# Where the input norm's weights are multiplied in: onto W_in by GpSimd, or onto the transposed rows by VectorE

## The chip, the core and the metric

The kernel runs on one core of a Trainium2 chip. The metric is the device time of one execution in microseconds.

## The reference

Two layers of an encoder trunk, on one sequence of 512 rows of 1024 numbers. What the change touches is the first step of a layer:

```python
h = rmsnorm(x, attn_norm_g[l])          # x * rsqrt(mean(x*x) + eps) * g
proj = einsum('bsd,de->bse', h, w_in)   # 1024 x 2464 columns for all mixers
aq, ak, av, bq, bk, bv, cq, ckv, ckr = split(proj)
kv = einsum('bsr,re->bse', rmsnorm(ckv, kv_norm_g), w_ukv)
vc = kv[..., C_NOPE_DIM:]               # values of the latent heads
```

Sixteen heads follow (six dilated, five differential, five latent), an output projection added to x, and a layer of 16 expert networks that each take 64 rows. The product of h with W_in does not depend on where the vector g is multiplied in: on W_in's rows or on the columns of x.

## The kernel before

A layer is one call of `attention` and then the router and the experts. `attention` loads W_in in seven pieces (`plan`) into three ring slots and works on it in 22 chunks. Chunks 0 to 13 are feature-major: up to 128 columns of W_in are the stationary operand and the 512 transposed rows stream past them, 24 passes of 128x512. Chunks 14 to 21 are token-major and make the values of the dilated and differential heads.

To reach the accuracy of full float32 with the faster format, both operands are cut in a high and a low part. `split` (L330 to L343) cuts a chunk of W_in: ScalarE casts it (L339), VectorE subtracts the cast from the original (L340). `turn_x` (L345 to L353) transposes a tile of x on TensorE into PSUM (L349), half a tile a bank; ScalarE casts it to `xh` (L352), VectorE subtracts to `xl` (L353). Each chunk is the sum of three products: high by high, high weights by low rows, low weights by high rows.

The vector g lies in `gcol`, one number a partition for each of the eight blocks of 128 inputs. `weigh` (L321 to L328) multiplies it onto a chunk of W_in in place, on GpSimd, two chunks ahead of its split. The factor of a row, 1/rms, is made by `row_norms` (squares on ScalarE, L359; the statistic `v` on VectorE, L362; a power on GpSimd, L176) and multiplied in later, when results are read.

Behind each feature-major chunk VectorE, GpSimd and ScalarE rotate it: `raw` (L404) reads PSUM, a shuffle (L406) and a product with the sines (L409) run on VectorE, a product with the cosines (L408) on GpSimd, then the sum `roped` (L410), the cast `hi` (L461) and the difference `lo` (L462). The latent heads need norms of their own columns: `c_sums` and `c_scale` (L450 writes `cqn`), hooked behind chunks 4 and 6. `c_values`, hooked behind chunk 7, makes the latent values from `cqn` (L455) and copies them out (L456). The up-projection of the first latent head (L530 to L532) follows chunk 8.

TensorE, VectorE, ScalarE, GpSimd and SyncE (SP) each run their instructions in a fixed order that the scheduler makes when the program is built; an instruction that waits holds up all behind it on its engine. `heat` issues matmuls on the identity, whose results nothing reads, between the transposes. PSUM has eight banks, handed out in turn. SP issues the loads of W_in and the stores of the rotated parts.

In the expert stage all weights are streamed from HBM, 1408 KB at a time, into tiles that lie where attention's tiles lay.

Of the kernel before, what the change touches and what calls it, by code (L numbers as in the profile page):

```python
# [11 lines left out]
F32 = mybir.dt.float32  # L12
# [5 lines left out]
ALU = mybir.AluOpType  # L18
# [4 lines left out]
P = 128  # L23
S = 512
# [3 lines left out]
KD = D // P  # L28
# [28 lines left out]
EARLY = [[(0, 1)], [(1, 1), (2, 1)], [(3, 1)], [(4, 1)], [(5, 1)], [(6, 1)], [(7, 1)], [], []]  # L57
END_ON = 'avavav'
MARK_AT = 6
FIRST_MARKS = 2  # L60
SCATTER_AT = (2, 4)
HALVED = 8
# [29 lines left out]
PB = 9  # L92
# [37 lines left out]
def body(ctx, tc, x_in, pos, w_in, w_uq, w_ukv, w_out, w_gate, w_up, w_down, gatt, gfin, params, consts, band, sel, out):  # L130
    nc = tc.nc
# [7 lines left out]
    def nm(s):  # L139
        uid[0] += 1  # L140
        return f"{s}_{uid[0]}"

    def bank():
        return pp.tile([P, 512], F32, tag="ps", name=nm("ps"))
# [13 lines left out]
    gcol = cp.tile([P, L, KD], F32, name="gcol")  # L158
# [97 lines left out]
    def attention(l, ap, wk, op):  # L256
# [5 lines left out]
        ukv = ap.tile([P, 5, P], F32, name="ukv")  # L262
# [14 lines left out]
        xl = [wk.tile([P, 4, S], F32R, tag="st", bufs=4, name=nm("xl")) for _ in range(2)]  # L277
# [14 lines left out]
        chunks = [(gi, cols, range(KD)) for gi, (_, _, parts) in enumerate(plan) for cols in parts]  # L292
        feature_major = len(chunks)
        chunks += [(gi, ((0, plan[gi][1]),), range(k, k + 2)) for gi in (5, 6) for k in range(0, KD, 2)]
        loaded = []

        def fetch():
            if len(loaded) < len(plan):
                c0, n, _ = plan[len(loaded)]
                v = slot(f"s{(len(loaded) + 2) % RING}")[:, : KD * n].rearrange("p (k f) -> p k f", k=KD)  # L300
                cuts = (0, 128, n) if not loaded else (0, n)
                for a, b in zip(cuts, cuts[1:]):
                    tc.keep_in_program_order(nc.sync.dma_start(v[:, :, a:b], w_in[l, :, c0 + a : c0 + b].rearrange("(k p) f -> p k f", p=P)))
                    if l == 0 and not loaded and a == 0:
                        for t in range(NT):
                            tc.keep_in_program_order(nc.sync.dma_start(x[:, t, :], x_in[t * P : (t + 1) * P, :]))
                loaded.append(v)
# [10 lines left out]
        nc.sync.dma_start(bandt, band)  # L318
        fetch()

        def weigh(i):  # L321

            if i < len(chunks):
                gi, cols, ks = chunks[i]
                for a, m in cols:
                    v = loaded[gi][:, ks[0] : ks[-1] + 1, a : a + m]
                    g = gcol[:, l, ks[0] : ks[-1] + 1].unsqueeze(2).to_broadcast([P, len(ks), m])
                    tc.keep_in_program_order(nc.gpsimd.tensor_tensor(v, v, g, op=ALU.mult))  # L328

        def split(i):  # L330
            gi, cols, ks = chunks[i]
            if i > 0 and chunks[i - 1][0] != gi and gi + 2 >= len(loaded):
                fetch()
            n = sum(m for _, m in cols)
            w = wk.tile([P, 2 * KD * P], F32R, tag=f"pt{SPLIT_IN[i]}", bufs=1, name=nm("w"))[:, : 2 * len(ks) * n].rearrange("p (c k f) -> p c k f", c=2, k=len(ks))
            o = 0
            for a, m in cols:
                src = loaded[gi][:, ks[0] : ks[-1] + 1, a : a + m]
                nc.scalar.copy(w[:, 0, :, o : o + m], src)  # L339
                nc.vector.tensor_tensor(w[:, 1, :, o : o + m], src, w[:, 0, :, o : o + m].bitcast(F32), op=ALU.subtract)  # L340
                o += m
            weigh(i + 2)
            return w, o  # L343

        def turn_x(t):  # L345
            for h in range(2):
                pt = bank()
                for k in range(4):
                    nc.tensor.transpose(pt[:, k * P : (k + 1) * P], x[:, t, (h * 4 + k) * P : (h * 4 + k + 1) * P], ident)  # L349
                pv = pt.rearrange("p (k s) -> p k s", k=4)  # L350
                hv = xh[:, h * 4 : h * 4 + 4, t * P : (t + 1) * P]
                nc.scalar.copy(hv, pv)  # L352
                nc.vector.tensor_tensor(xl[h][:, :, t * P : (t + 1) * P], pv, hv.bitcast(F32), op=ALU.subtract)  # L353

        def row_norms():
            ss = wk.tile([P, 8], F32, tag="rr", bufs=RB, name=nm("ss"))[:, :NT]
# [8 lines left out]
        def spread(r):  # L365

            b = bank()
            for t in range(NT):
                nc.tensor.transpose(b[:, t * P : (t + 1) * P], r[:, t : t + 1].to_broadcast([P, P]), ident)
            nc.scalar.copy(rb, b)  # L370

        def heat(n):

            if n:
                b = bank()
                for _ in range(n):
                    nc.tensor.matmul(b[:, :P], ident, ident, start=True, stop=True)

        weigh(0)
        if l > 0:  # L380
            weigh(1)
            ready = split(0)
        for t in range(NT):
            heat(START[l][t])
            turn_x(t)
        if l == 0:
            weigh(1)
            ready = split(0)
        heat(START[l][NT])
        rstd = row_norms()  # L390
# [21 lines left out]
        cqn = [cqn2[:, 0], tab_c[0:64, 0], cqn2[:, 1]]  # L412
# [39 lines left out]
        def c_values():  # L452
            for t in range(NT):
                pv = bank()
                nc.tensor.matmul(pv[:, :320].rearrange("p (h c) -> p h c", h=5), cqn[2][:, t * P : (t + 1) * P], ukv[:, :, 64:128], start=True, stop=True)  # L455
                nc.scalar.copy(vC[:, t, :], pv[:, :320])  # L456

        def halves(roped):
# [267 lines left out]
                events[n].pop(0)[2]()  # L726
            events.pop(n, None)

        hooks = {4: c_sums, 5: get_lam, 6: c_scale, 7: c_values}
        hooks.update({i: lambda i=i: step(i - feature_major) for i in range(8, feature_major)})  # L730

        pump(100)
# [1 line left out]
        for i in range(len(chunks)):  # L734
            w, m = ready
            if i < feature_major:
                b = bank()
                passes = ((0, lambda k: xh[:, k, :]), (0, lambda k: xl[k // 4][:, k % 4, :]), (1, lambda k: xh[:, k, :]))
                order = [(j, k) for j in range(3) for k in range(KD)] if i == 0 else [(j, k) for k in range(KD) for j in range(3)]
                for n, (j, k) in enumerate(order):  # L740
                    nc.tensor.matmul(b[:m], w[:, passes[j][0], k, :m], passes[j][1](k), start=(n == 0), stop=(n == 3 * KD - 1))  # L741
            else:
                ks = chunks[i][2]
                if ks[0] == 0:
                    acc = [bank() for _ in range(NT)]
                for kk, k in enumerate(ks):
                    for t in range(NT):
                        q = slice(t * P, (t + 1) * P)
                        for j, (c, xs) in enumerate(((0, xh[:, k, q]), (1, xh[:, k, q]), (0, xl[k // 4][:, k % 4, q]))):
                            nc.tensor.matmul(acc[t][:, :m], xs, w[:, c, kk, :], start=(k == 0 and j == 0), stop=(k == KD - 1 and j == 2))  # L750
                    if kk == 0:
                        step(i - feature_major)
            if i + 1 < len(chunks):
                ready = split(i + 1)
            if i == 2:
                tab_ab = wk.tile([P, 4, S], F32, tag="pt1", bufs=1, name="tab_ab")
                tabs += [tab_ab[:, 0], tab_ab[:, 1], tab_ab[:, 2], tab_ab[:, 3], tab_c[:, 0], tab_c[:, 1]]
                if l == 0:
                    make_tables(tabs, *sines())
                else:  # L760
                    for q in range(6):
                        rows = slice(0, P) if q < 4 else slice(64, 96)
                        nc.scalar.dma_start(tabs[q][rows], tab_d[q, rows])
            if i < feature_major:
                held.append((posts[i], b))
                if i == 1:
                    spread(rstd)
                if i > 0:
                    for fn, b in held:
                        fn(b)  # L770
                    held = []
            elif ks[-1] == KD - 1:
                dst = vB if chunks[i][0] == 5 else vA
                for t in range(NT):
                    nc.scalar.activation(dst[:, t, :], acc[t][:, :m], AF.Copy, scale=rstd[:, t : t + 1])
            if i in hooks:
                hooks[i]()
        late = op.tile([P, 16, 256], F32R, tag="big", name="oh")
# [82 lines left out]
    for l in range(L):  # L861
        with ExitStack() as es:
            ap = es.enter_context(tc.tile_pool(name=f"at{l}", bufs=1, reuse_waits="tile"))
            wk = es.enter_context(tc.tile_pool(name=f"wk{l}", bufs=2, reuse_waits="tile"))
            op = es.enter_context(tc.tile_pool(name=f"op{l}", bufs=1, side="right", reuse_waits="tile"))
            product, work = attention(l, ap, wk, op)
            spots = {}

# [180 lines left out]
            t = NT - 1  # L1049
# [33 lines left out]
        with tc.tile_pool(name=f"fx{l}", bufs=1, reuse_waits="tile") as fx, tc.tile_pool(name=f"fw{l}", bufs=2, side="right", reuse_waits="tile") as fw:  # L1083
# [129 lines left out]
            for p in range(8):  # L1213
                acc = []
                for w in (w_gate, w_up):
                    bs = [bank() for _ in cuts]
                    acc.append(bs)
                    for k in range(KD):
# [7 lines left out]
                        if w is w_gate and k in SCATTER_AT and pending is not None:  # L1226
                            scatter(*pending, 2 * SCATTER_AT.index(k))
                        if w is w_up and k == FIRST_MARKS and p == 0:
                            ohs[0] = marks(0)
                        if w is w_gate and k == MARK_AT and p < 7:  # L1230
                            ohs[p + 1] = marks(p + 1)
# [3 lines left out]
                for g, u, (q0, qn) in zip(acc[0], acc[1], cuts):  # L1235
                    hv = hh[:, :, q0 : q0 + qn].rearrange("p j q -> p q j")
# [14 lines left out]
                for lo in range(0, NJ * D, FF):  # L1251
# [3 lines left out]
                    while e < hi:  # L1255
                        j, h = e // D, e % D // 512
# [143 lines left out]
```

## Time and profile before

| | us |
|---|---|
| median of three runs | 1974.07 |
| lowest and highest run | 1973.97, 1975.56 |
| the profiled execution, its own time | 1974.58 |
| its span, from the first to the last instruction | 1972.8 |

| engine | busy us | share of the span | instructions |
|---|---|---|---|
| TensorE (PE), matmuls | 1754.5 | 89% | 8894 |
| VectorE (DVE) | 739.9 | 38% | 1467 |
| ScalarE (ACT) | 425.0 | 22% | 881 |
| GpSimd (POOL) | 290.8 | 15% | 276 |

The shares are means over stages that differ. The projection and the heads of layer 0 lie in the first 340 us, those of layer 1 between about 985 and 1310 us; the expert stages between and behind them move 420 GB/s or more for most of their time. A line like L340 is line 340 of the kernel before.

### The profile page before, as it was taken

To read this page: it belongs to the slowest core of one execution; us is meant where nothing else is said; L and a number is where in the kernel's file an instruction comes from. 1 tells how busy PE (TensorE), PEld (TensorE's weight loads), DVE (VectorE), ACT (ScalarE), POOL (GpSimd) and SP (SyncE) were. 2 spreads that over 40 slices of the span, in tenths; PEclk is the share of its full clock that TensorE was granted. 3 is DMA by queue.
4 is the path that set the end of the run, shared out by engine and by line. 5 is a ranking of instruction groups with operands and counts; after the bars stand their busy time and mean duration, and the time that the engine had idled before them with its cause. 6 is when DMAs were issued, how large, how long until landed. Compare 5 with 4: busy or idle time off the path is not lost.

```text
span 1972.8 us, 22329 instructions
## 1 busy us (share of the span) xinstructions
PE 1754.5 (89%) x8894; PEld 918.0 (47%) x8894; DVE 739.9 (38%) x1467; ACT 425.0 (22%) x881; POOL 290.8 (15%) x276
## 2 busy tenths in 40 slices
PE   8889999898998988888898899998998988888887
PEld 6667666433333333333386756753333433333323
DVE  7886966111111111211178778551211211211112
ACT  4226972000000000000042379411000000000001
POOL 4552431000000000000055344200000000000000
PEclk9999999999999999999999999999999999999999
DMA  6755548899999999999947546488999999999995
GB/s 220 197 164 91 121 142 322 317 402 423 424 425 424 425 424 425 424 423 425 406 128 224 141 82 158 161 334 346 425 425 424 424 425 424 425 425 424 425 424 245
DMA packets 102473, 646.72 MB, mean 328 GB/s; under 512 B 11009, under 2 KB 28161, under 8 KB 53217
## 3 DMA queue, kind: packets, MB, share of 16 engines
q1 hardware_dynamic: 88336, 606.34, 76.7%
q0 software_dynamic: 11968, 35.02, 7.6%
q10 hardware_dynamic: 2064, 3.93, 0.6%
q8 instruction: 70, 1.15, 0.2%
q14 instruction: 35, 0.28, 0.0%
HBM read 616.55 MB, written 27.39 MB: 326 GB/s over the span
## 4 chain that ended last, share of the span: by engine, by line
DMA 39%; PE 37%; DVE 14%; issue 5%; ACT 3%; POOL 1%; SPq 0%; DVEq 0%; ACTq 0%; POOLq 0%
DMA xslot<-in_w_up_dram 13%; PE ps L1222 10%; DMA xslot<-in_w_gate_dram 10%; PE ps L1259 8%; DMA xslot<-in_w_down_dram 7%; PE ps L840 4%; DMA rows<-xrow_d,slots 3%; DMA slot<-in_w_gate_dram 3%; DMA slot<-in_w_down_dram 3%; PE ps L750 2%; PE ps L741 2%; PE ps L659 2%; PE ps L642 2%; DVE sm L591 1%; DVE sw L409 1%
## 5 line engine op out<-in xcount | busy, mean ns | idle before, releaser
L1222 PE MATMUL ps<-xslot,xe 128*64 128x506 f32 (+1 forms) x2400 | 515.8, 575 | 25.5 <-DMA xslot<-in_w_up_dram 13.3
L1222 PEld LDWEIGHTS ps<-xslot,xe 128*64 128x64 f32 x2400 | 167.0, 140 | 347.3 <-issue 288.5
L1259 PE MATMUL ps<-xslot,hx 128*64 128x512 f32 (+3 forms) x1392 | 248.6, 506 | 22.3 <-DMA xslot<-in_w_down_dram 18.4
L1238 DVE TENSOR_TENSOR hx<-ps,hx 128x506 f32<-128x506 f32 (+1 forms) x48 | 42.9, 957 | 473.9 <-PE ps L1222 473.9
L1259 PEld LDWEIGHTS ps<-xslot,hx 128*64 128x64 f32 x1392 | 94.2, 137 | 164.5 <-issue 123.4
L1189 ACT ACTIVATE hx<-ps,gates 128x512 fp32r<-128x512 f32 x32 | 20.2, 683 | 674.7 <-PE ps L1259 674.7
L1169 POOL DMA_INDIRECT rows<-xrow_d,slots x14 | 13.8, 984 | 985.2 <-DVE oh L1162 913.7
L1190 DVE SCALAR_TENSOR_TENSOR hx<-ps,gates,hx 128x512 fp32r<-128x512 f32 x32 | 22.6, 747 | 344.6 <-ACT hx L1189 344.6
L1222 PE MATMUL ps<-slot,xe 128*64 128x506 f32 (+1 forms) x648 | 141.8, 573 | 7.7 <-DMA slot<-in_w_gate_dram 6.0
L741 PE MATMUL ps<-xh,w 128*128 128x512 f32 (+1 forms) x448 | 142.6, 400 | 3.1 <-DVE w L340 2.4
L1200 DVE TENSOR_TENSOR x<-ps,x 128x512 f32<-128x512 f32 x112 | 69.6, 684 | 161.9 <-PE ps L1198 161.9
L598 ACT ACTIVATE P<-ps,sm 128x512 f32<-128x512 f32 x168 | 116.4, 703 | 41.1 <-DVE sm L591 40.0
L1170 ACT ACTIVATE rows<-rows,slots 128x1024 f32<-128x1024 f32 x14 | 16.1, 1147 | 446.0 <-DMA rows<-xrow_d,slots 446.0
L328 POOL TENSOR_TENSOR slot<-slot,gcol 128x1024 f32<-128x1024 f32 (+4 forms) x46 | 88.1, 1929 | 119.8 <-PE ps L1275 109.8
L741 PEld LDWEIGHTS ps<-xh,w 128*128 128x128 f32 (+1 forms) x448 | 83.3, 187 | 25.9 <-DVE w L340 3.3
L1222 PEld LDWEIGHTS ps<-slot,xe 128*64 128x64 f32 x648 | 45.3, 139 | 93.6 <-issue 75.8
L1177 PE MATMUL ps<-ident,rows 128*128 128x128 f32 x112 | 26.7, 417 | 66.5 <-ACT rows L1170 66.5
L741 PE MATMUL ps<-xl,w 128*128 128x512 f32 (+1 forms) x224 | 85.7, 393 | 0.0
L591 DVE TENSOR_REDUCE sm<-ps 128x1 f32<-128x512 f32 x120 | 78.9, 681 | 8.1 <-PE ps L576 5.7
L642 PE MATMUL ps<-ident,P 128*128 128x128 f32 x512 | 78.0, 275 | 0.3 <-ACT P L598 0.3
L1259 PE MATMUL ps<-slot,hx 128*64 128x512 f32 (+3 forms) x400 | 71.6, 497 | 6.2 <-DMA slot<-in_w_down_dram 4.7
L750 PE MATMUL ps<-w,xh 128*128 128x320 f32 (+1 forms) x256 | 65.9, 342 | 10.4 <-DVE w L340 10.4
(280 smaller groups left out, 2299.1 us busy)
## 6 DMA issues: line engine op xcount, KB each, us to landing
xslot<-in_w_gate_dram SPq DMA_DIRECT2D x100, 1408.0 KB, 26.2
xslot<-in_w_up_dram SPq DMA_DIRECT2D x100, 1408.0 KB, 27.1
xslot<-in_w_down_dram SPq DMA_DIRECT2D x100, 1408.0 KB, 27.0
slot<-in_w_gate_dram SPq DMA_DIRECT2D x28, 1408.0 KB, 27.0
slot<-in_w_down_dram SPq DMA_DIRECT2D x28, 1408.0 KB, 27.0
slot<-in_w_up_dram SPq DMA_DIRECT2D x26, 1408.0 KB, 27.4
slot<-in_w_in_dram SPq DMA_DIRECT2D x8, 1536.0 KB, 6.8
st<-bst_d POOLq DMA_DIRECT2D x40, 256.0 KB, 4.7
```

The source lines that it names most:

```text
L328: tc.keep_in_program_order(nc.gpsimd.tensor_tensor(v, v, g, op=ALU.mult))
L591: nc.vector.tensor_reduce(mn, ps, axis=AX.X, op=ALU.min)
L598: nc.scalar.activation(e, ps, AF.Exp, bias=mn, scale=-1.0, accum_out=lcol)
L642: nc.tensor.transpose(b[:, kc * P : (kc + 1) * P], e[:, kc * P : (kc + 1) * P], ident)
L659: nc.tensor.matmul(o[64 * i : 64 * i + 64], heads[2 * m + i][4][:, kc, :], pts[i][:, kc, :], start=(kc == 0), stop=(kc == NT - 1))
L741: nc.tensor.matmul(b[:m], w[:, passes[j][0], k, :m], passes[j][1](k), start=(n == 0), stop=(n == 3 * KD - 1))
L750: nc.tensor.matmul(acc[t][:, :m], xs, w[:, c, kk, :], start=(k == 0 and j == 0), stop=(k == KD - 1 and j == 2))
L840: nc.tensor.matmul(blocks[t][1 + h], o, w[h], start=(i == 0), stop=(i == 3 * KD - 1))
L1200: nc.vector.tensor_tensor(xv, b, xv, op=ALU.add)
L1222: tc.keep_in_program_order(nc.tensor.matmul(b[64 * i : 64 * i + 64, : qn * NJ], xe[:, k, 64 * i : 64 * i + 64], ws[i][:, q0 * NJ : (q0 + q ...
L1238: nc.vector.tensor_tensor(hv, u[:, : qn * NJ].rearrange("p (q j) -> p q j", j=NJ), hv, op=ALU.mult)
L1259: tc.keep_in_program_order(nc.tensor.matmul(bs[h][64 * i : 64 * i + 64, e % 512 : e % 512 + z - e], hT[:, j, 64 * i : 64 * i + 64], ws[i][ ...
```

## The change

The multiplication by g leaves GpSimd and W_in: `weigh` and its calls go. `turn_x` multiplies g onto the transposed rows instead: VectorE reads the PSUM bank, multiplies and writes a new SBUF tile `gx`; ScalarE's cast and VectorE's subtraction then both read `gx`. The first chunk takes its three products in another order, low weights ahead of low rows. `c_values` moves from behind chunk 7 to behind chunk 9, and its matmuls are pinned there in program order.

```diff
+VALUES_AT = 9
...
-        def weigh(i):
-
-            if i < len(chunks):
-                gi, cols, ks = chunks[i]
-                for a, m in cols:
-                    v = loaded[gi][:, ks[0] : ks[-1] + 1, a : a + m]
-                    g = gcol[:, l, ks[0] : ks[-1] + 1].unsqueeze(2).to_broadcast([P, len(ks), m])
-                    tc.keep_in_program_order(nc.gpsimd.tensor_tensor(v, v, g, op=ALU.mult))
...
-            weigh(i + 2)
             return w, o
 
         def turn_x(t):
+
             for h in range(2):
                 pt = bank()
                 for k in range(4):
                     nc.tensor.transpose(pt[:, k * P : (k + 1) * P], x[:, t, (h * 4 + k) * P : (h * 4 + k + 1) * P], ident)
-                pv = pt.rearrange("p (k s) -> p k s", k=4)
+                gx = wk.tile([P, S], F32, tag="P", bufs=PB, name=nm("gx")).rearrange("p (k s) -> p k s", k=4)
+                g = gcol[:, l, h * 4 : h * 4 + 4].unsqueeze(2).to_broadcast([P, 4, P])
                 hv = xh[:, h * 4 : h * 4 + 4, t * P : (t + 1) * P]
-                nc.scalar.copy(hv, pv)
-                nc.vector.tensor_tensor(xl[h][:, :, t * P : (t + 1) * P], pv, hv.bitcast(F32), op=ALU.subtract)
+                nc.vector.tensor_tensor(gx, pt.rearrange("p (k s) -> p k s", k=4), g, op=ALU.mult)
+                nc.scalar.copy(hv, gx)
+                nc.vector.tensor_tensor(xl[h][:, :, t * P : (t + 1) * P], gx, hv.bitcast(F32), op=ALU.subtract)
...
-        weigh(0)
         if l > 0:
-            weigh(1)
             ready = split(0)
...
-                nc.tensor.matmul(pv[:, :320].rearrange("p (h c) -> p h c", h=5), cqn[2][:, t * P : (t + 1) * P], ukv[:, :, 64:128], start=True, stop=True)
+                tc.keep_in_program_order(nc.tensor.matmul(pv[:, :320].rearrange("p (h c) -> p h c", h=5), cqn[2][:, t * P : (t + 1) * P], ukv[:, :, 64:128], start=True, stop=True))
...
-        hooks = {4: c_sums, 5: get_lam, 6: c_scale, 7: c_values}
+        hooks = {4: c_sums, 5: get_lam, 6: c_scale}
...
-                order = [(j, k) for j in range(3) for k in range(KD)] if i == 0 else [(j, k) for k in range(KD) for j in range(3)]
+                order = [(j, k) for j in (0, 2, 1) for k in range(KD)] if i == 0 else [(j, k) for k in range(KD) for j in range(3)]
...
+            if i == VALUES_AT:
+                c_values()
```

The scheduler places the instructions anew. SP's order stays as it was. On ScalarE at the start of layer 0 the order before was the following, where `junk` are the squares, `xh` the casts of the rows and `w` the casts of W_in:

```order
L352 CAST xh<-ps_253 128x4x128
L359 ACTIVATE junk_295,ss_292<-x 128x1024
L352 CAST xh<-ps_267 128x4x128
L352 CAST xh<-ps_274 128x4x128
L359 ACTIVATE junk_297,ss_292<-x 128x1024
L339 CAST w_368<-slot_179 128x1024
L359 ACTIVATE junk_299,ss_292<-x 128x1024
```

In the change ScalarE has, at the same place (its line numbers are those of the changed kernel, here and below):

```order
L331 CAST w_296<-slot_179 128x1024
L353 ACTIVATE junk_305,ss_304<-x 128x1024
L353 ACTIVATE junk_307,ss_304<-x 128x1024
L353 ACTIVATE junk_309,ss_304<-x 128x1024
L353 ACTIVATE junk_311,ss_304<-x 128x1024
L331 CAST w_380<-slot_179 128x1024
L346 CAST xh<-gx_219 128x4x128
L346 CAST xh<-gx_228 128x4x128
```

All four squares and the second weight cast now stand ahead of the first cast of the rows. VectorE, before, in the same stretch, where `v` is the statistic made from the four squares and `tabw` the angles of the sine tables:

```order
L353 TENSOR_TENSOR xl_177<-ps_267,xh 128x4x128
L353 TENSOR_TENSOR xl_178<-ps_274,xh 128x4x128
L340 TENSOR_TENSOR w_368<-slot_179,w_368 128x1024
L362 TENSOR_SCALAR v_301<-ss_292 128x4
L211 CAST tabw_192<-tabw_192 128x128
```

VectorE in the change:

```order
L332 TENSOR_TENSOR w_296<-slot_179,w_296 128x1024
L356 TENSOR_SCALAR v_313<-ss_304 128x4
L345 TENSOR_TENSOR gx_219<-ps_214,gcol 128x512
L345 TENSOR_TENSOR gx_228<-ps_223,gcol 128x512
L345 TENSOR_TENSOR gx_237<-ps_232,gcol 128x512
L347 TENSOR_TENSOR xl_177<-gx_219,xh 128x4x128
L347 TENSOR_TENSOR xl_178<-gx_228,xh 128x4x128
L347 TENSOR_TENSOR xl_177<-gx_237,xh 128x4x128
L345 TENSOR_TENSOR gx_246<-ps_241,gcol 128x512
```

The statistic moved ahead of the rows' steps, and each `xl` has a `gx` ahead of it, three by three. TensorE around the latent values in layer 0, before, where `w_704` is chunk 7 and `w_769` chunk 8:

```order
L741 MATMUL ps_742<-xh,w_704 128x512
L455 MATMUL ps_794<-ukv,cqn 128x320
L455 MATMUL ps_797<-ukv,cqn 128x320
L455 MATMUL ps_800<-ukv,cqn 128x320
L455 MATMUL ps_803<-ukv,cqn 128x320
L741 MATMUL ps_806<-xh,w_769 128x512
```

TensorE in the change, where `w_823` is chunk 9 and `w_873` chunk 10:

```order
L732 MATMUL ps_848<-xh,w_823 128x512
L446 MATMUL ps_891<-ukv,cqn 128x320
L446 MATMUL ps_894<-ukv,cqn 128x320
L446 MATMUL ps_897<-ukv,cqn 128x320
L446 MATMUL ps_900<-ukv,cqn 128x320
L732 MATMUL ps_907<-xh,w_873 128x512
```

The four matmuls stand two chunks later, and behind the up-projection of the first latent head.

## Rows read from the trace of the kernel before

**Rows 1.** Busy us of each engine (instructions) in a stretch, granted clock, DMA.
```profile
76.00:80.00 4.00, 0.91 (x2) 0.72 (x3) 4.00 (x7) 0.20 (x1) 2.36 (x2) 0.50 0.35 87
```

**Rows 2.** Waits of TensorE, 0 to 180 us: total us, times, longest.
```profile
PE ps L455 <- DVE cqn L450: 7.2, 1, 7.2
PE ps L750 <- DVE w L340: 5.2, 1, 5.2
PE ps L532 <- DVE raw L404: 3.2, 1, 3.2
...
PE ps L741 <- DVE w L340: 2.4, 2, 1.6
PE ps L248 <- ACT wide_w L239: 1.6, 2, 1.4
```

**Rows 3.** Timeline of TensorE, layer 1, with idle time before and its releaser.
```profile
1047.87 4.57 PE L455 MATMUL ps<-ukv,cqn 128*128 128x320 f32 x8 [6.50 <-DVE cqn L450]
...
1096.26 1.66 PE L532 MATMUL ps<-cqn,ukv 128*64 128x512 f32 x2 [3.22 <-DVE raw L404]
...
1110.42 0.63 PE L750 MATMUL ps<-w,xh 128*128 128x320 f32 x1 [5.20 <-DVE w L340]
```

**Rows 4.** The chain that ended last, layer 0: start us, us, what.
```profile
79.09 4.27 PE ps L455 x8
...
141.30 3.22 PE ps L750 x11
144.97 3.51 PE ps L750 x24
```

**Rows 5.** Timeline of VectorE and GpSimd: start us, us, instruction.
```profile
50.26 3.75 DVE L340 TENSOR_TENSOR w<-slot,w 128x1024 fp32r<-128x1024 f32 x1
...
51.02 1.91 POOL L328 TENSOR_TENSOR slot<-slot,gcol 128x1024 f32<-128x1024 f32 x1
```

**Rows 6.** Groups on VectorE, 36 to 142 us: busy us, mean ns, idle before.
```profile
L340 DVE TENSOR_TENSOR w<-slot,w 128x1024 fp32r<-128x1024 f32 x10 | 16.6, 1660 | 1.5 <-ACT w L339 1.4
L409 DVE TENSOR_TENSOR sw<-sw,tab_ab 128x512 f32<-128x512 f32 x11 | 13.1, 1188 | 0.1
L410 DVE TENSOR_TENSOR roped<-rc,sw 128x512 f32<-128x512 f32 x11 | 11.8, 1075 | 0.9 <-DVE sw L409 0.5
```

**Rows 7.** Groups on GpSimd, whole execution and 0 to 142 us.
```profile
L328 POOL TENSOR_TENSOR slot<-slot,gcol 128x1024 f32<-128x1024 f32 (+4 forms) x46 | 88.1, 1929 | 119.8 <-PE ps L1275 109.8
...
L408 POOL TENSOR_TENSOR rc<-raw,tab_ab 128x512 f32<-128x512 f32 x11 | 15.9, 1448 | 33.6 <-DVE raw L404 29.7 <-DVE ljunk L395 3.9
```

**Rows 8.** One line's instructions: shortest, median, longest in ns.
```profile
L1178 DVE TENSOR_TENSOR xe<-ps,pgf x28: 679/683/689, 410.4 to 1844.5; 128x512 f32<-128x512 f32 x28
```

**Rows 9.** Timeline at the start of layer 0: start us, us, instruction.
```profile
8.64 1.05 ACT L359 ACTIVATE junk<-x 128x1024 f32<-128x1024 f32 x1
...
13.84 1.07 ACT L352 CAST xh<-ps 128x512 fp32r<-128x512 f32 x2
...
14.08 1.06 PE L377 MATMUL ps<-ident 128*128 128x128 f32 x8
...
14.89 2.09 PE L741 MATMUL ps<-xh,w 128*128 128x512 f32 x8
...
16.93 1.23 DVE L340 TENSOR_TENSOR w<-slot,w 128x1024 fp32r<-128x1024 f32 x1 [1.18 <-ACT w L339]
```

**Rows 10.** The loads of x: first and last issue, time to landing.
```profile
L306 SPq DMA_DIRECT2D x<-in_x_dram x4: 432/580/663, 1.7 to 3.4; - x4
...
DMA to landing us min/median/max: 5.2/6.3/7.3
```

**Rows 11.** Start of layer 1: timeline rows and one of the chain.
```profile
988.42 1.28 DVE L1283 TENSOR_TENSOR x<-ps,x 128x512 f32<-128x512 f32 x2
...
989.94 4.28 DVE L353 TENSOR_TENSOR xl<-ps,xh 128x512 fp32r<-128x512 f32 x7 [0.24 <-ACT xh L352]
...
994.42 11.37 PE ps L741 x48
```

More of the change, by code (lines that the diff above doesn't have):

```diff
@@ L386, in attention @@
         if l == 0:
-            weigh(1)
             ready = split(0)
```

## The prediction

> **What bounds the kernel now.** I read the views in this order: busy time by stretch, to find stages whose engines have different limits; TensorE's waits in the projection stage of each layer; the chain around those waits; then VectorE and GpSimd instruction by instruction. In four microseconds of layer 0's projection stage TensorE is busy for 0.91 us, VectorE for all 4.00 and GpSimd for 2.36, and the granted clock is 0.50, the lower of its two levels [rows 1]. So this stage is not bound by TensorE, although TensorE is the busiest engine of the whole page. Its waits name the cause: in layer 0 three long ones, 7.2 us for `cqn`, 5.2 us for a split weight, and 3.2 us for `raw`, whose reading frees a PSUM bank [rows 2]; in layer 1 the same three, 6.5, 5.2 and 3.2 us [rows 3]. All end on VectorE.
>
> Each costs time afterwards too. The eight passes of the values matmuls behind the first wait take 4.27 us, at the clock of [rows 1]; at the full one they would take half, so 2.1 us are lost. Behind the second, 11 passes take 3.22 us where 24 later ones take 3.51 [rows 4]: 1.6 us lost.
>
> Why is VectorE late? Its weight split at 50.26 takes 3.75 us and ends about 1 us after GpSimd's weighting multiply, which starts at 51.02 and takes 1.91 [rows 5]; an undisturbed split of that size takes 1.23 [rows 9]. The groups give a total for layer 0 [rows 6]: ten splits take 16.6 us where 10 x 1.23 = 12.3 would do, eleven rope products 13.1 and eleven rope sums 11.8 where 11 x 0.68 = 7.5 would do for each (0.683 is an undisturbed product of that size [rows 8]). Together that is 14.2 us too much, and smaller groups stall in the same way.
>
> **The change part by part.** *GpSimd's 46 multiplies go*, 23 a layer, mean 1.93 us [rows 7]. Nothing takes their place in W_in's path: its pieces go from the load straight to the split. Not all of the 14.2 us are theirs, because the rope's own GpSimd multiply remains, about a dozen a layer at 1.45 us [rows 7], and stalls VectorE too. I give it a third of its time, 12 x 0.45, some 5 us, as an estimate: part of it runs beside steps that read PSUM. That leaves 9 us in the three groups, and I take 13 with the smaller groups and with ScalarE's casts that waited for a weighted piece. Bounds: 8, if the smaller groups give nothing, and 18, if the rope's multiply stalls nothing.
>
> *VectorE gains eight multiplies a layer* (gx, 128x512, one input in PSUM, a broadcast weight). The same form stands in the expert stage at 0.683 us [rows 8]; back to back such steps take 0.61, seven in 4.28 [rows 11]. That is 4.9 us a layer, all of it ahead of the first projection matmul, which needs the high part of every tile.
>
> *Start of layer 0.* ScalarE's order now puts all four squares ahead of the casts, and VectorE's puts the statistic `v`, which waits for all four, ahead of gx. The last tile of x is issued at 3.4 us and lands at most 7.3 us later [rows 10], so by 10.7; a square takes 1.05 us [rows 9], and with its read-out and the step to `v` I put `v` at 12.2. The eighth gx is then VectorE's 14th step (8 gx, 6 xl): 12.2 + 14 x 0.61 = 20.7, plus some 0.6 us in which the first xl waits for a cast that stands behind a weight cast, plus the last cast, 1.07 / 2 = 0.53 [rows 9]: 21.9. Before, the first projection matmul started at 14.89 [rows 9], so it comes 7.0 us later. TensorE's last filler ends at 15.1 [rows 9]; it idles 6.8 us, and I add 1.8 us of lower clock, between the 1.6 and 2.1 above. Given back are the 2.4 and 1.6 us that TensorE waits in this stretch for splits and for the sine tables [rows 2], since both are ready in time for a TensorE that is 8 us late. Net -4.8 us.
>
> *Start of layer 1.* gx can start when the last residual is written, 988.42 + 1.28 = 989.7 [rows 11]. The eighth gx is ready after 8 gx, 7 xl and one split: 15 x 0.61 + 1.2 = 10.3, so at 1000.0; some 0.3 us of waits for casts and the last cast make it 1000.8. By then four of the eight first products are done, since the tiles of the first half are ready 2.4 us earlier; against the start at 994.42, with 48 passes in 11.37 us or 0.24 each [rows 11], the loss is 1000.8 - 994.42 - 4 x 0.24 = 5.4 us, and 0.8 for a lower clock: -6.2 us. The first chunk's new pass order, low weights ahead of low rows, keeps the eighth xl off this path.
>
> *The values matmuls move behind the tenth chunk.* The wait for `cqn` then has two chunks to hide under: TensorE goes straight on to chunk 8, whose weights were split long before. The wait and its clock go: 7.2 + 2.1 us and, with eight passes in 4.57 us [rows 3], 6.5 + 2.3, together 8.8. If VectorE is later than I think, the next to wait is the up-projection, which needs the same `cqn` 24 passes or 5.7 us later.
>
> *The other two waits* go if VectorE gains at least what TensorE gains before them: 3.2 + 5.2, and 1.7 + 1.6 of lower clock (1.7 taken like its neighbours), 11.7 us a layer.
>
> So TensorE's own sum is 9.3 + 11.7 - 4.8 = 16.2 in layer 0 and 8.8 + 11.7 - 6.2 = 14.3 in layer 1. VectorE caps it: its last split of the stage comes 13 us of stalls earlier, and the 1.6 us of clock behind that wait go as well, about 15; what the late start leaves on VectorE and what ScalarE's earlier casts save I set against each other. I take 15.5 and 14: **29.5 us**. Everything behind (heads, output projection, router, experts) starts from TensorE's and VectorE's progress here, and the expert loads start when attention's tiles come free, so the gain should reach the end undiminished.
>
> A row against a rule: the xl subtraction now has two SBUF inputs (gx, xh) where it had one. Splits with two such inputs are what stalls in the trace, up to 3.75 us [rows 5]. In xl's place GpSimd has only fills, one row load and a power, so I add nothing. The Trainium skill, "SBUF — State Buffer" (Who interferes with whom), says that a VectorE instruction with two SBUF inputs and a GpSimd instruction that reads SBUF exclude each other for the whole instruction. By it, xl could lose one power, about 1 us a layer as an estimate, and the sum would be 27.5; the trace agrees with the exclusion, and no row of the kernel before shows xl in this form.
>
> **The numbers.** The profiled execution took 1974.58 us, 0.5 above the median of the runs. 1974.58 - 29.5 gives 1945.1; I say 1945.
>
> **The rivals.**
> *(A) The stall passes to the rope multiply.* GpSimd is now always free, so each rope multiply starts right with its raw tile and meets VectorE's next split or product in full. For: it takes 1.45 us and I count a third [rows 7]. Against: some of these meetings are paid already. Price: another third, some 5 us a layer on a VectorE that caps the sum: 1955.
> *(B) Only the values wait goes*; VectorE keeps TensorE waiting at the other two points. Gain 9.3 - 4.8 + 8.8 - 6.2 = 7: 1967. It needs VectorE to win less than 6 us a layer; the groups of [rows 6] speak against it.
> *(C) Slower.* VectorE is on the chain for the whole stage and the late start stays on it to the end, while the stalls turn out to belong to the rope's multiply and stay; moving the values only moves the wait to the up-projection. Place: the eighth xl and everything behind it in VectorE's queue. Price: 6 us a layer, less some 2 for the values matmuls at the full clock: 1983. It decides if the stalls fall by less than the 4.9 us of gx.
> *(D) The gain is lost behind the stage*, because the heads start from something else, such as their own loads: 1974.
> *(E) More*: no lower clock at the two starts (2.6 us) and no cap by VectorE (1.1), with 5 us more from casts and banks that come free earlier: 1936.
>
> **How the numbers follow.** Forecast (1938 to 1950) 0.50; A 0.22; B 0.10; E 0.05; C 0.08; D 0.05. The range 1935 to 1962 holds the forecast, A and E, and the bounds of the stalls (8 and 18 in place of 13, two layers, 10 us either way, the upper side cut by TensorE's own sum). A measurement tells about 0.2%, 4 us, from no change. Faster: 0.50 + 0.22 + 0.10 + 0.05 = 0.87; same 0.05; slower 0.08.
>
> **What would show it.** Right: no wait of TensorE on `cqn`; those on `raw` and on the late split under 1.5 us; rope products at 0.7 to 0.9 us on average instead of 1.19 [rows 6]; the first projection matmul of layer 0 near 22 us. Wrong: a new wait of over 3 us at the up-projection (C), rope sums that still take over 1 us (A), or a projection stage shorter by 30 us with an unchanged end (D).

## The result and the profile after

The changed kernel takes **1948.64 us** (median; 1948.13 to 1949.72 over 4 runs) against 1974.82 for the kernel before, measured beside it: ratio 0.9864, 95% interval 0.9852 to 0.9876. That is 26.2 us less where 29.5 were forecast. The profiled execution has a span of 1947.6 us, 25.2 less than the span before.

TensorE's waits, 0 to 180 us of the changed kernel (total us, times, longest), answer to [rows 2]:

```profile
PE ps L732 <- ACT xh L346: 6.8, 1, 6.8
...
PE ps L741 <- DVE w L332: 1.2, 1, 1.2
```

The waits for `cqn` and for `raw` are gone, that for the late split fell from 5.2 to 1.2 us, and the new first wait is the late start (line 732 is the projection matmul, line 741 the token-major one). In layer 1 the same two are left, 4.7 and 1.2 us. VectorE's groups, 36 to 130 us (busy us, mean ns, idle before), answer to [rows 6] (line 332 is the weight split, lines 400 and 401 the rope's product and sum):

```profile
L332 DVE TENSOR_TENSOR w<-slot,w 128x1024 fp32r<-128x1024 f32 x11 | 16.6, 1511 | 3.6 <-ACT w L331 3.6
L400 DVE TENSOR_TENSOR sw<-sw,tab_ab 128x512 f32<-128x512 f32 x11 | 8.6, 782 | 0.1
...
L401 DVE TENSOR_TENSOR roped<-rc,sw 128x512 f32<-128x512 f32 x11 | 7.5, 685 | 0.6
```

By the prediction's own reckoning (11 x 1.23 for splits, 7.5 for the others) 3.1 + 1.1 + 0 = 4.2 us too much are left of 14.2 (the stretch of [rows 6] has ten splits, this one eleven). GpSimd's remaining group in that stretch is unchanged [rows 7]:

```profile
L399 POOL TENSOR_TENSOR rc<-raw,tab_ab 128x512 f32<-128x512 f32 x11 | 15.9, 1446 | 40.8 <-DVE raw L395 31.8 <-DVE ljunk L386 5.0 <-DMA bst_d<-hi 3.9
```

The starts of the two layers, timeline of VectorE, ScalarE and TensorE [rows 9, 11]:

```profile
11.81 0.17 DVE L356 TENSOR_SCALAR v<-ss 128x4 f32<-128x4 f32 x1 [4.18 <-ACT junk L353]
...
20.67 1.22 ACT L346 CAST xh<-gx 128x512 fp32r<-128x512 f32 x2 [1.79 <-DVE gx L345]
...
21.34 6.49 PE L732 MATMUL ps<-xh,w 128*128 128x512 f32 x16 [6.82 <-ACT xh L346]
...
986.51 7.24 PE L732 MATMUL ps<-xh,w 128*128 128x512 f32 x17 [4.71 <-ACT xh L346]
```

Behind each wait the first 16 or 17 passes take 0.41 to 0.43 us each, where [rows 11] has 0.24; the granted clock is 0.81 on average from 987 to 1002 us and 1.00 in the 58 us after that.

Where the time came from shows when the two chains (start us, us, what) are laid side by side. Before:

```profile
271.13 3.58 PE ps L659 x16
...
291.51 3.58 PE ps L659 x16
...
342.88 34.75 issue
378.56 9.67 DMA rows<-xrow_d,slots
...
971.72 11.99 PE ps L1259 x68
...
1288.45 7.22 PE ps L840 x31
...
1941.58 12.16 PE ps L1259 x68
```

After, the same steps:

```profile
255.81 3.63 PE ps L650 x16
263.23 11.35 DMA slot<-in_w_out_dram
277.01 3.65 PE ps L650 x16
...
328.61 36.31 issue
365.84 9.72 DMA rows<-xrow_d,slots
...
959.84 7.27 PE ps L1252 x40
...
1264.26 7.22 PE ps L833 x31
...
1916.80 12.14 PE ps L1252 x68
```

The lead is 15.3 us at the end of layer 0's heads (271.13 to 255.81), 14.5 behind the load of W_out, 14.3 at the router, 12.7 behind it and 11.9 when layer 0's experts end. Layer 1's stage adds 12.3 (24.2 at 1264.26), and the lead is 24.8 at the last row.

### The profile page after: what moved, and what is told of

It is laid out like the page before. It is cut to its first block, busy times and chain, and to the rows that moved or that the text cites. A ratio compares the mean times of both kernels' runs of the same rounds, so it can differ in the third digit from the quotient of the medians.

```text
span 1947.6 us, 22276 instructions
## 1 busy us (share of the span) xinstructions
PE 1747.3 (90%) x8894; PEld 914.8 (47%) x8894; DVE 709.2 (36%) x1483; ACT 426.2 (22%) x881; POOL 203.2 (10%) x230
## 4 chain that ended last, share of the span: by engine, by line
DMA 43%; PE 38%; DVE 9%; issue 5%; ACT 3%; POOL 1%; SPq 0%; DVEq 0%; ACTq 0%; POOLq 0%
DMA xslot<-in_w_up_dram 13%; DMA xslot<-in_w_down_dram 10%; PE ps L1215 9%; DMA xslot<-in_w_gate_dram 8%; PE ps L732 7%; PE ps L1252 6%; DMA slot<-in_w_gate_dram 6%; PE ps L833 4%; DMA rows<-xrow_d,slots 4%; PE ps L741 2%; PE ps L650 2%; PE ps L633 1%; DVE sm L582 1%; DMA slot<-in_w_down_dram 1%; PE ps L493 1%
## 5 line engine op out<-in xcount | busy, mean ns | idle before, releaser
L1215 PE MATMUL ps<-xslot,xe 128*64 128x506 f32 (+1 forms) x2400 | 515.9, 575 | 29.1 <-DMA xslot<-in_w_up_dram 16.6
L732 PE MATMUL ps<-xh,w 128*128 128x512 f32 (+1 forms) x448 | 147.6, 414 | 11.5 <-ACT xh L346 11.5
L641 ACT COPY pt<-ps 128x512 f32<-128x512 f32 x118 | 68.8, 604 | 25.8 <-PE ps L633 25.5
L633 PEld LDWEIGHTS ps<-ident,P 128*128 128x128 f32 x512 | 62.5, 141 | 24.4 <-ACT P L589 7.0
```

The costliest lines, as they stand in the source:

```text
L633: nc.tensor.transpose(b[:, kc * P : (kc + 1) * P], e[:, kc * P : (kc + 1) * P], ident)
L641: nc.scalar.copy(dv, bv)
L1215: tc.keep_in_program_order(nc.tensor.matmul(b[64 * i : 64 * i + 64, : qn * NJ], xe[:, k, 64 * i : 64 * i + 64], ws[i][:, q0 * NJ : (q0 + q ...
```

## The experiments

**One part undone: the values back behind the eighth chunk.**

```diff
-VALUES_AT = 9
+VALUES_AT = 7
```

> The changed kernel with the values matmuls back behind the eighth chunk. If the wait for cqn was a thing of its own, as the prediction's sum has it (9.3 us in layer 0 and 8.8 in layer 1), most of that comes back: 1962 to 1967 us. If it was only VectorE's lateness, cqn is now there before chunk 7 ends (in the changed kernel's trace at 76 us, against 81.5 for the end of the chunk) and nothing waits: 1947 to 1950 us, no wait on cqn over 0.5 us.

Measured: 1949.5 us, ratio to the kernel before 0.9865 (0.985 to 0.988), the same as with the move. TensorE does not wait for `cqn` in layer 0, and in layer 1 (waits, 960 to 1180 us) it waits 1.0 us for it:

```profile
PE ps L446 <- DVE cqn L441: 1.0, 1, 1.0
```

Once GpSimd's multiplies are gone, the move is worth nothing that this measurement can tell.

**The same part alone, in the kernel before.**

```diff
-        hooks = {4: c_sums, 5: get_lam, 6: c_scale, 7: c_values}
+        hooks = {4: c_sums, 5: get_lam, 6: c_scale}
...
+            if i == VALUES_AT:
+                c_values()
```

> The kernel before with the values matmuls moved behind the tenth chunk and nothing else changed. If the wait for cqn is a cost of its own, 18 us go: 1956 to 1960 us. If VectorE is what bounds the stage, TensorE meets VectorE a chunk later and the waits for raw and for the late split grow by what the wait for cqn loses: 1968 to 1975 us, and those two waits together at 12 us or more in layer 0 (8.4 before).

Measured: 1974.21 us, ratio 0.9991 (0.9982 to 1.0). TensorE's waits, 0 to 180 us, became

```profile
PE ps L742 <- DVE w L341: 6.7, 3, 4.2
PE ps L751 <- DVE w L341: 3.9, 1, 3.9
PE ps L533 <- DVE raw L405: 2.8, 1, 2.8
```

The 7.2 us for `cqn` are gone and the time is not: TensorE runs a chunk ahead and meets VectorE at the splits of the projection chunks (line 742; 6.7 us where [rows 2] has 2.4). The expectation named the wrong place, since the late split and `raw` together fell from 8.4 to 6.7. The wait for `cqn` was where VectorE's lateness showed, not its cost.

**GpSimd as busy as before, with nobody waiting for it.**

```diff
+        spin = vA.rearrange("p t f -> p (t f)")
+        nc.vector.memset(spin[:, : KD * P], 1.0)
...
+                    v = spin[:, : len(ks) * m].rearrange("p (k f) -> p k f", k=len(ks))
+                    g = gcol[:, l, ks[0] : ks[-1] + 1].unsqueeze(2).to_broadcast([P, len(ks), m])
+                    tc.keep_in_program_order(nc.gpsimd.tensor_tensor(v, v, g, op=ALU.mult))
```

> The changed kernel with GpSimd's 46 weighting multiplies put back in their places, but on the still empty tile of values vA, so that no split waits for them. If VectorE was slowed because the two engines hinder each other, the stalls return though nobody reads the result: rope products and sums at 1.1 us or more on average, 1963 to 1980 us. If the splits were late because they waited for weighted pieces, nothing returns: 1948 to 1953 us, rope products under 0.85 us.

Measured: 1986.94 us, ratio 1.0057 (1.0044 to 1.0071), 38 us more than the changed kernel, 11 us more than the kernel before, and beyond what was expected. VectorE's groups, 36 to 140 us:

```profile
L342 DVE TENSOR_TENSOR w<-slot,w 128x1024 fp32r<-128x1024 f32 x11 | 19.1, 1734 | 3.6 <-ACT w L341 3.6
L415 DVE TENSOR_TENSOR roped<-rc,sw 128x512 f32<-128x512 f32 x11 | 12.8, 1166 | 0.6
L414 DVE TENSOR_TENSOR sw<-sw,tab_ab 128x512 f32<-128x512 f32 x11 | 12.4, 1128 | 0.1
...
L411 DVE STREAM_SHUFFLE sw<-raw 128x512 f32<-128x512 f32 x11 | 8.2, 745 | 0.0
L409 DVE SCALAR_TENSOR_TENSOR raw<-ps,rb 128x512 f32<-128x512 f32 x6 | 4.1, 682 | 0.0
```

The stalls of [rows 6] are back, in the steps that have two inputs in SBUF; the shuffle, with one, and `raw`, whose first input is in PSUM, keep their 0.74 and 0.68 us. No result passes between the two engines here, so what slows VectorE is GpSimd's work itself, and only where a step has two inputs in SBUF. The start of layer 0 (timeline of VectorE and GpSimd) shows it in one picture:

```profile
14.59 5.57 DVE L358 TENSOR_TENSOR xl<-gx,xh 128x512 fp32r<-128x512 f32 x3 [0.79 <-ACT xh L357]
...
21.88 1.88 DVE L358 TENSOR_TENSOR xl<-gx,xh 128x512 fp32r<-128x512 f32 x3
...
13.12 6.50 POOL L330 TENSOR_TENSOR vA<-vA,gcol 128x1024 f32<-128x1024 f32 x3
```

Three `xl` take 5.57 us beside three GpSimd multiplies; the next three, behind them, take 1.88. The profile books all of it as busy time of VectorE.

**An earlier start, first try: the squares behind the casts.**

```diff
-        if l > 0:
-            ready = split(0)
+        ready = split(0)
         for t in range(NT):
...
-        if l == 0:
-            ready = split(0)
```

> The changed kernel with layer 0's first split traced ahead of the turned rows, so that the four squares and the statistic v stand behind the casts of the rows on ScalarE and behind xl on VectorE. If the late start of layer 0 costs what the prediction says (-4.8 us, most of it in the 6.8 us for which TensorE waits), the first projection matmul comes at 15 to 18 us and the kernel takes 1942 to 1946 us. If VectorE caps the stage, the earlier start turns into waits further on: 1947 to 1950 us.

Measured: 1950.82 us, ratio 0.9872 (0.9857 to 0.9888): no gain, and the first projection matmul came at 22.18 us, not at 15 to 18. ScalarE's timeline says why:

```profile
13.78 1.04 ACT L331 CAST w<-slot 128x1024 fp32r<-128x1024 f32 x1 [6.59 <-DMA slot<-in_w_in_dram]
14.73 1.65 ACT L346 CAST xh<-gx 128x512 fp32r<-128x512 f32 x3
```

The cast of the second chunk's weights stood ahead of the casts of the rows and waited 6.6 us for its load. The edit did not test what it was made for.

**Second try: that cast out of the way too** (the edit above, and this).

```diff
+                hi = nc.scalar.copy(w[:, 0, :, o : o + m], src)
...
+                if i in (1, 2):
+                    tc.keep_in_program_order(hi)
+                    tc.keep_in_program_order(lo)
```

> As the run with the late squares, and the casts and subtractions of the second and third split pinned behind the squares and behind v, so that no load of weights stands ahead of the casts of the rows. Layer 0's first projection matmul should come at 15.5 to 17.5 us (21.3 in the changed kernel) and layer 1's some 2 us earlier relative to its last residual. If the two late starts are still paid at the end, as the prediction's -4.8 and -6.2 have it, 1940 to 1945 us. If VectorE caps both stages, the time stays at 1947 to 1951 us and TensorE waits over 3 us more at later splits or at raw.

Measured: 1953.18 us, ratio 0.9885 (0.987 to 0.99). The first projection matmul came at 16.59 us, as expected, and the kernel lost time. TensorE's waits, 0 to 180 us:

```profile
PE ps L249 <- ACT wide_w L240: 10.0, 1, 10.0
```

The sine angles, some 10 us of small VectorE steps, stood behind `v`, and `v`, which waits for the squares, now came at 21.77 us instead of 11.81. So neither reading of the expectation came about: another chain, the angles, had been hidden by the late start. Layer 1's wait stayed at 4.7 us.

**What the weighting costs in its new place: the weight left out.**

```diff
-                gx = wk.tile([P, S], F32, tag="P", bufs=PB, name=nm("gx")).rearrange("p (k s) -> p k s", k=4)
...
-                nc.vector.tensor_tensor(gx, pt.rearrange("p (k s) -> p k s", k=4), g, op=ALU.mult)
-                nc.scalar.copy(hv, gx)
-                nc.vector.tensor_tensor(xl[h][:, :, t * P : (t + 1) * P], gx, hv.bitcast(F32), op=ALU.subtract)
+                nc.scalar.copy(hv, pv)
+                nc.vector.tensor_tensor(xl[h][:, :, t * P : (t + 1) * P], pv, hv.bitcast(F32), op=ALU.subtract)
```

> The changed kernel with the norm's weight left out of the computation: no gx, ScalarE and VectorE read the transposed rows from PSUM as before the change, and GpSimd's multiplies stay away. It shows what the weighting still costs in its new place. The prediction's two late starts, 4.8 and 6.2 us, give 1936 to 1940 us; if VectorE is still the bound of the stage, its eight multiplies of 4.9 us a layer count in full beside them, 1930 to 1936 us; if they are hidden, 1945 us or more.

Measured: 1933.31 us, ratio 0.9786 (0.9773 to 0.9799), 15 us below the changed kernel. From its chain:

```profile
16.41 11.34 PE ps L729 x48
...
319.93 36.25 issue
...
950.72 11.99 PE ps L1249 x68
973.76 11.38 PE ps L729 x48
...
1272.15 34.60 issue
```

Against the changed kernel's 328.61 the weighting costs 8.7 us in layer 0; in layer 1 the stretch from the last expert to the router is 1272.15 - 950.72 = 321.4 here and 1287.82 - 959.84 = 328.0 there, so 6.6 us.

**What the rope's own GpSimd multiply still costs: the cosine product left out.**

```diff
-            nc.gpsimd.tensor_tensor(rc[lo:hi], raw[lo:hi], cos[lo:hi], op=ALU.mult)
...
-            nc.vector.tensor_tensor(dst, rc[lo:hi], sw[lo:hi], op=ALU.add)
+            nc.vector.tensor_tensor(dst, raw[lo:hi], sw[lo:hi], op=ALU.add)
```

> The changed kernel with the rope's product by the cosine left out of the computation (GpSimd's last multiplies of 128x512, a dozen a layer, gone; the sum reads raw instead). The prediction gave 5 us a layer of remaining stalls to them. If VectorE still bounds the stage, 8 to 10 us go: 1938 to 1942 us. If TensorE is the bound by now and VectorE runs ahead of it, under 3 us go: 1946 to 1949 us, though the splits fall from 1.51 to 1.25 us on average.

Measured: 1944.94 us, ratio 0.9842 (0.9828 to 0.9855): some 4 us, between the two theories. VectorE's groups, 36 to 130 us, are all at their undisturbed length:

```profile
L332 DVE TENSOR_TENSOR w<-slot,w 128x1024 fp32r<-128x1024 f32 x11 | 13.4, 1215 | 3.8 <-ACT w L331 3.6
...
L398 DVE TENSOR_TENSOR sw<-sw,tab_ab 128x512 f32<-128x512 f32 x11 | 7.5, 685 | 0.1
```

Layer 0's splits and products alone lose (16.6 - 13.4) + (8.6 - 7.5) = 4.3 us of stalls, and the same groups in layer 1 lose some 3 us; about half of both was still paid at the end. In the chain of the changed kernel VectorE's steps fill the time from 98 to 127 us (rows below, with the fillers). Here TensorE's passes fill it:

```profile
92.70 22.28 PE ps L730 x96
```

**The first chunk's passes in the old order.**

```diff
-                order = [(j, k) for j in (0, 2, 1) for k in range(KD)] if i == 0 else [(j, k) for k in range(KD) for j in range(3)]
+                order = [(j, k) for j in range(3) for k in range(KD)] if i == 0 else [(j, k) for k in range(KD) for j in range(3)]
```

> The changed kernel with the first chunk's passes back in the order of before (low rows ahead of low weights). The last low part of the rows is ready some 1.3 us after the last high part, and eight passes take at least 1.8 us, so it should not matter: 1948 to 1950 us. If it does matter, the wait is under 1.5 us a layer: up to 1952 us.

Measured: 1947.86 us, ratio 0.9866 (0.985 to 0.9881). The measurement tells no difference.

**Only TensorE's clock: fillers in the two waits.**

```diff
-START = [[6, 0, 2, 6, 4], [2, 0, 0, 4, 2]]
+START = [[6, 0, 2, 6, 26], [2, 0, 0, 4, 18]]
```

> The changed kernel with more filler matmuls behind the last transposes (22 more in layer 0, 14 more in layer 1, some 5.8 and 3.7 us in the 6.8 and 4.7 us in which TensorE waits for the casts of the rows). They only keep TensorE from idling. If the lower clock after the wait is paid at the end (layer 0's first 16 passes took 6.49 us where 16 at the full clock take 3.9; layer 1's 48 took 14.42 where 11.38 do), 2.6 + 3.0 us go: 1941 to 1945 us, and the granted clock right behind the first pass is 1.00. If VectorE caps the stage instead, 1947 to 1950 us.

Measured: 1944.21 us, ratio 0.9842 (0.9829 to 0.9856), 4.4 us below the changed kernel. Timeline of TensorE (2.00 us of the wait are left), and the chain's row for the first chunks:

```profile
21.23 3.04 PE L732 MATMUL ps<-xh,w 128*128 128x512 f32 x12 [2.00 <-ACT xh L346]
```

```profile
21.23 11.36 PE ps L732 x48
```

The 48 passes of the first two chunks take 11.36 us instead of 13.90, and the granted clock from 15 to 36 us is 1.00. VectorE's work is the same in both kernels, and it still bounds the end of the stage. In both chains it takes over at the same `raw` and leads up to the last weight split; in the changed kernel

```profile
98.03 0.70 DVE raw L395
...
127.32 1.88 PE ps L741 x11
```

and with the fillers

```profile
95.39 0.70 DVE raw L395
...
124.68 1.88 PE ps L741 x11
```

The stretch is 29.3 us long in both and only starts 2.6 us earlier. So TensorE bounds the first part of the stage and VectorE the last, one behind the other. Not all of the gain is surely the fillers': in the traces layer 0's piece at the router, described at the end, is 1.7 us shorter here than in the changed kernel (34.60 and 36.31).

**All weighted rows ahead of the first `xl`, angles ahead of `v`, tables pinned behind the third chunk.**

```diff
+        rows = [v.rearrange("p t f -> p (t f)")[:, S * j : S * j + S] for v, n in ((vA, 3), (vB, 2), (vC, 2)) for j in range(n)]
...
+                gx = rows[2 * t + h]
...
+        for h in range(2):
+            for t in range(NT):
...
+                tc.keep_in_program_order(nc.vector.tensor_tensor(lv, rows[2 * t + h], hv.bitcast(F32), op=ALU.subtract))
...
+        pump(100)
+        second = split(1, True)
         rstd = row_norms()
```

> The changed kernel with the start of both layers in another order: the eight weighted pieces kept in still empty tiles (vA, vB, vC), so that VectorE makes all of them before the first xl; squares, the second weight split and v behind the casts of the rows; the sine angles ahead of v, and the table matmuls pinned behind the third chunk. Layer 0's first projection matmul should come at 15 to 16 us (21.3 in the changed kernel) and layer 1's some 3 us earlier. By the run without weights the starts cost 8.7 and 6.6 us; if they can be hidden, 1936 to 1941 us. If the next late work takes their place (the angles and the sine tables, as in the run with the rows first, or the second split), 1945 to 1952 us.

Measured: 1940.54 us, ratio 0.9825 (0.9812 to 0.9838). The first projection matmul starts at 15.11 us and the clock holds; then TensorE meets the tables (timeline):

```profile
36.58 7.89 PE L249 MATMUL ps<-wide_w,sl 128*128 128x512 f32 x12 [4.05 <-ACT wide_w L240]
```

**The tables one chunk later, and eight fillers in layer 1** (on top of the last edit).

```diff
-            if i == 2:
+            if i == (3 if l == 0 else 2):
                 tab_ab = wk.tile([P, 4, S], F32, tag="pt1", bufs=1, name="tab_ab")
...
-                if i > 0:
+                if i > 0 and (l > 0 or i != 2):
```

> As the run with gx first, with layer 0's sine tables a chunk later (their matmuls behind the fourth chunk, and what follows the third chunk waiting for them), and eight filler matmuls more at layer 1's start. In the run with gx first TensorE waited 4.1 us for the tables, their 12 matmuls took 7.89 us at the lower clock where 5.3 would do, and layer 1's first 48 passes took 12.93 us instead of 11.38. If TensorE is what bounds both stages now, some 4.1 + 2.6 + 1.5 = 8 us go: 1931 to 1935 us. If VectorE, which gets the tables and two chunks' products later, is the next to be waited for, 1937 to 1941 us, with a wait for raw or a split of over 2 us.

Measured: **1935.69 us**, ratio 0.9797 (0.9784 to 0.9811), 13 us below the changed kernel and 40 below the one before: the best version of this study. The tables' row and the first chunks of both layers (timeline, then chain):

```profile
37.68 5.31 PE L249 MATMUL ps<-wide_w,sl 128*128 128x512 f32 x12
```

```profile
14.88 11.40 PE ps L739 x48
...
975.28 11.36 PE ps L739 x48
```

Of the 8 us named, some 5 came; two waits of 1.1 and 1.4 us for the next weight splits, behind the tables, took part of the rest.

## Why the prediction was nearly right

*Forecast 1945 us in 1935 to 1962; measured 1948.64.* The direction and the cause hold: VectorE's stalls beside GpSimd went, and with them TensorE's waits. None of the rivals came about as such: the rope's multiply stalls VectorE by 4.2 us in layer 0, not by twice what was assumed (A), the waits for `raw` and the late split fell together with that for `cqn` (B), layer 0's stalls fell by ten us against the 4.9 of `gx` (C), and of layer 0's gain only 3.4 us were lost behind its stage (D).

*The multiplies go: right.* Nine of the 14.2 us in the three groups were to go; ten went. The idle multiplies show the cause, which the prediction had only argued. The Trainium skill, "SBUF — State Buffer" (Who interferes with whom), which the prediction weighed, says that VectorE instructions with two SBUF inputs and GpSimd instructions that read SBUF exclude each other; the trace with the idle multiplies agrees (1.86 us for each of three `xl` beside them, 0.69 at the median in the changed kernel). In the changed kernel `xl` lost nothing (0.694 us at most): layer 0's power ran at 12.07 us, ahead of the first `xl`, and layer 1's at 993.80, behind the last. So the 2 us by which the rule could have lowered the sum were not lost.

*"The values matmuls move": wrong in its place, right in the sum.* 9.3 and 8.8 us were credited to the move. Undone, it changes nothing that can be measured; alone, it brings 0 to 0.2%. The wait did go, so the sum stands, but the multiplies took it away and not the move: that the sum came out is luck as far as the move goes. The same holds for the "given back" 4.0 us at layer 0's start: the kernel without the weight starts at 16.41 us, not 8 us late, and has not those waits either.

*Start of layer 0.* First matmul forecast at 21.9 us, measured 21.34; the lower clock forecast at 1.8 us, measured 13.90 - 11.36 = 2.5. *Start of layer 1.* Forecast -6.2, of which 0.8 for the clock. The first matmul came 4.0 us later against the lead of 11.9, and the first 48 passes took 14.42 us instead of 11.37 [rows 11]: 7.1, with the clock's share mis-sized almost fourfold. Without the 4.0 given back, the two starts were forecast at 8.8 and 6.2 us, and the run without the weight, which itself starts 1.5 us later than the kernel before, measures 8.7 and 6.6.

*VectorE's cap: the right place, the wrong form.* In layer 0 VectorE's last split lets TensorE go at 127.32 us instead of 141.30 [rows 4], 14.0 us earlier, and the eleven passes behind it take 1.88 us instead of 3.22: together 15.3, the whole lead, where the prediction had 13 and 1.6. But it set TensorE's sum beside VectorE's and took the smaller, as if one engine bounded the whole stage. The chain has both, TensorE up to 98 us and VectorE behind it. So a faster start gains (the fillers) and fewer stalls gain (no cosine product), each by itself.

*"The gain should reach the end undiminished": the step that failed.* Layer 0's stage gave 15.3 us (15.5 forecast), but only 11.9 reached layer 1. 0.8 went at the load of W_out, which became the chain's longest piece there, and 0.2 between it and the router; why was not tried out. 1.6 went at the router, at a lower clock. The two rows run from the start of the chain's "issue" piece to the first matmul on the experts' weights (us; busy us of PE, PEld, DVE, ACT and POOL; granted clock; DMA), in the kernel before and the changed one:

```profile
342.88:350.93 8.05, 6.54 (x30) 2.72 (x28) 5.35 (x23) 0.69 (x2) 0.00 (x0) 0.83 0.88 351
```

```profile
328.61:338.22 9.61, 7.86 (x28) 4.02 (x28) 5.43 (x23) 0.69 (x2) 0.00 (x0) 0.54 0.72 299
```

The stretch is 1.56 us longer, with VectorE's work the same. The remaining 0.8 went in the experts, where transfers of weights fill the chain. In layer 1 the stage gave 12.3 where TensorE's own sum was 14.3 (14 taken): the start cost 0.9 more, and a last wait of 1.2 us for a split stayed, which the sum had counted as gone.

## What to carry to other kernels

A long busy time of VectorE on a step with two SBUF inputs, beside a busy GpSimd, was a wait in disguise here, and idle copies of GpSimd's work on an unused tile told whether data or the engines' meeting was the cause. Waits that end on one late engine are one cost: put it down to the engine, not to each wait, and undo the parts of a change one by one before any is given credit. Two engines can bound one stage one behind the other; then the chain tells where each leads, and taking the smaller of two sums does not. Work that moved to the start of a stage cost its wait and then the clock behind it; fillers took back the second at once, and whoever pulls the start forward must look for the chain that the late start had hidden.

## What the runs showed that was not expected

The chain's "issue" piece at the router has one of two lengths. Over two layers of the kernel before, the changed one and the eleven variants it was 34.5 to 34.9 us 18 times and 36.1 to 36.3 us 8 times, in either layer. Its length goes with the granted clock: in the first 8 us of the piece it was 0.81 to 0.99 in all 18 short ones and 0.50 in seven of the 8 long ones; in the eighth (idle multiplies, layer 1) it was 0.93 there and 0.86 in the 8 us behind. What sets it is not shown, nor whether it changes between executions of one kernel, since each was traced once. It differs between kernels whose edits lie far away from it, so differences of 1.5 us between two variants need a look at this piece first; the fillers' gain is one of them.

GpSimd's multiplies together with the new start make a kernel that is slower than before (1986.94 us): the new start is a price, and it is the multiplies' going that pays it back.
